# A hybrid decoder layer on one core: eight plain products in two groups of the down projection, its sums on VectorE, and the norm weight in the weight splits of the front

## The chip, the core and the metric

The kernel runs on one core of one Trainium2 chip. The metric is the device time of one launch in microseconds (us). The engines that matter are TensorE (PE in the rows; PEld are its weight loads), VectorE (DVE), ScalarE (ACT) and GpSimd (POOL). Loads and stores are DMA transfers, issued from the queue of SyncE (SP) for the most part. TensorE's clock is granted at one of two levels, 1.2 or 2.4 GHz; a stretch's granted clock is a share of full speed.

## The reference

One inference step of a decoder layer: 1024 prompt tokens and 8 sample tokens, 1024 channels, all in float32. Cut to what matters here:

```python
proj = rms_norm(h, norm_mix) @ w_in          # 1024 -> 3360; then sparse attention and gated DeltaNet
h = h + concat(o_nsa, o_gdn) @ w_out
gate, up = split(rms_norm(h, norm_ffn) @ w_gate_up)
h = h + (silu(gate) * up) @ w_down           # 2816 -> 1024, the down projection
y = rms_norm(h, norm_final)
# rms_norm(x, g) = x * rsqrt(mean(x * x) + 1e-6) * g
```

## The kernel before, in words

**Numbers.** Every operand of a large product is kept as two reduced-precision tiles, a high part (a cast on ScalarE, or a copy) and a low part (the operand less its high part). A product is then three matmuls: high by high, high by low and low by high. So each operand costs one ScalarE copy and one subtraction, and the name `split` or `parts` marks the place. `q`, `wh`/`wl`, `xh`/`xl`, `C` are such pairs.

**The front** (`in_proj`, L288 on). The 1032 tokens lie in nine tiles `x`, 128 tokens each and 8 in the last. `normalise` loads a tile, squares and sums it on ScalarE (L309), finds the root on VectorE in some eleven small instructions (`rsqrt`, L196 to L201), multiplies the tile by root and norm weight `gmix` (L319 on VectorE for the first three tiles, L316 on ScalarE and L317 on GpSimd for the others), turns it in eight TensorE transposes (L325, `S<-K,x`, `K` holding the identity) and splits the result into `xh` and `xl` (L149, L150). `natural(pw, 3)` multiplies the tiles by 352 columns of `w_in`, 24 matmuls a tile (L359), from eight weight tiles `wraw` that it loads in two pieces each and splits into `wh` and `wl`. The main program steps `normalise` and `natural` in turns. After that `conv_channels` and `channel` (L276 to L290) multiply all tokens by twelve blocks of 128 columns: one load `ch_raw` (512 KB), one copy on ScalarE (L279), one subtraction on GpSimd (L280), 72 matmuls (L285).

**The down projection** (from L2070 on). `w_down` has 22 blocks of 128 rows; blocks 1 to 20 make five groups `g` of 512 rows, and in each group four pairs `i` of two output blocks, 20 pairs `v` in all. A pair is a product of 2 by 2 blocks by 2 by 2 blocks, and it is done with seven products in place of eight (`down_pair`, `ORDER`): sums and differences of blocks are formed first, of weights in `pair_weights`, of the tokens' blocks in `group_build` (its combinations are `T1` to `T4`). Each product is 12 matmuls of 258 columns (L1874, `Z`), 84 for a pair, and after each the sum so far is added to the result `acc` (tiles `hTa`, `hTb`) on VectorE; in group 0 four of seven go to ScalarE as copies. While pair `v` runs, the weights of pair `v + 1` are split and those of `v + 2` loaded, and one step after the other of the next group's `group_build` is done: the generator `steps` hands out 14 steps in each pair.

**Who does what there.** On ScalarE the high parts. On VectorE the low parts, the adds of the results, and two of the four weight sums. On GpSimd the two other weight sums, one of seven low parts (`part(12, 6, a12, G)`), all sums of tokens' blocks (`sub(..., eng=G)`), and the residual, eight adds of 1032 columns (`res`, `RES`). `last_weights` does four low parts on GpSimd for the piece that ends the kernel, `last_down` (L1911, L1916).

**The order.** In the front a scheduler orders each engine's instructions. From the output projection on, the wrapper `InOrder` (L74) keeps those of VectorE, ScalarE and GpSimd in the order of the program, so that one that waits holds back all behind it. All three record their instructions at L74; the tiles' names tell them apart.

## Time and profile before

| | |
|---|---|
| runs of the kernel | 1840.51, 1840.69, 1845.69 us; median 1840.69 |
| profiled execution | 1840.93 us |
| its span in the trace | 1839.2 us, so 1.7 us lie outside |
| mean granted clock | 0.972 |
| busy TensorE, VectorE, ScalarE, GpSimd | 1707.1, 1129.8, 822.3, 543.1 us |

The shares are means over stages that have different limits, so the stretches are read one by one: the front up to 73 us, the conv channels up to about 240 us, and the down projection from 1543.7 to 1798.8 us. In a row, `<-` after a duration names who ended the idle time before it, `x12` counts instructions, and a form such as `128x258` is partitions by elements.

### The profile page before, as it was taken

Reading aid. Unit: us, or ns where it says so; the run is one execution under the profiler, and the core shown is the slowest. Engines: PE = TensorE matmul, PEld = TensorE weight load, DVE = VectorE, ACT = ScalarE, POOL = GpSimd, SP = SyncE. Lnnn points to the kernel's source line nnn. Section 1 sums busy time; section 2 is a strip of 40 time slices with the busy share of each in tenths; the row PEclk is TensorE's granted clock in tenths of the full one; section 3 lists DMA queues with packets and bytes.
Section 4 is the critical chain, followed back from the end, with each engine's and each line's share of the span. In section 5 each row is a group of like instructions: output and inputs, shape, how many; then the busy total and the mean of one; then the engine's idle time right before and its main releaser. Section 6 shows DMA issues by size and latency. Waiting matters only on the chain.

```text
span 1839.2 us, 32099 instructions
## 1 busy us (share of the span) xinstructions
PE 1707.1 (93%) x12066; PEld 1504.6 (82%) x12066; DVE 1129.8 (61%) x2693; ACT 822.3 (45%) x1932; POOL 543.1 (30%) x511
## 2 busy tenths in 40 slices
PE   5999999989999899999999989999999998888898
PEld 4999989989876466555486589999999998888897
DVE  6559873677467555545534268444444447899976
ACT  5357632222355665558744454433333335433322
POOL 2324330221111221110143254322333234555540
PEclk8999999999989989999999999999999999999999
DMA  7226454764422563752344342323223224332212
GB/s 212 68 92 204 163 168 123 238 207 147 107 75 61 153 201 114 191 149 87 122 139 127 85 121 78 94 88 98 86 88 104 93 82 162 104 115 81 95 55 93
DMA packets 247554, 224.02 MB, mean 122 GB/s; under 512 B 76097, under 2 KB 226113, under 8 KB 245214
## 3 DMA queue, kind: packets, MB, share of 16 engines
q1 hardware_dynamic: 232516, 189.31, 33.2%
q0 software_dynamic: 7008, 22.11, 3.7%
q10 hardware_dynamic: 7874, 10.56, 1.8%
q8 instruction: 95, 1.56, 0.4%
q14 instruction: 61, 0.50, 0.1%
HBM read 148.95 MB, written 60.40 MB: 114 GB/s over the span
## 4 chain that ended last, share of the span: by engine, by line
PE 56%; DVE 8%; DMA 5%; ACT 3%; issue 1%; POOL 1%; SPq 1%; ACTq 0%; POOLq 0%; DVEq 0%
PE X L1722 12%; PE Z L1874 7%; PE V L1722 6%; PE O L1090 4%; PE g L1495 3%; PE Y L1722 3%; DVE q L74 3%; PE mm L1420 3%; PE S L1010 2%; PE X L1097 2%; PE S L1011 2%; DMA kx<-gx 2%; PE X L1100 2%; PE X L359 1%; PE Y L1916 1%
## 5 line engine op out<-in xcount | busy, mean ns | idle before, releaser
L74 POOL TENSOR_TENSOR q<-q,q 128x258 f32<-128x258 f32 (+3 forms) x130 | 159.8, 1240 | 212.3 <-DVE q L74 184.8
L74 DVE TENSOR_TENSOR q<-q,q 128x256 fp32r<-128x256 f32 (+5 forms) x231 | 168.8, 743 | 52.3 <-ACT q L74 50.6
L74 ACT CAST q<-q 128x256 fp32r<-128x256 f32 (+2 forms) x219 | 99.3, 485 | 169.3 <-DVE q L74 158.8
L1016 ACT ACTIVATE S<-S,nb 128x512 f32<-128x512 f32 (+4 forms) x256 | 119.6, 468 | 58.7 <-DVE nb L1014 54.7
L1014 DVE TENSOR_REDUCE nb<-S 128x1 f32<-128x512 f32 (+4 forms) x154 | 95.3, 637 | 53.2 <-PE S L1013 49.1
L1102 ACT ACTIVATE PF<-X 128x512 f32<-128x512 f32 (+1 forms) x148 | 85.6, 596 | 38.9 <-PE X L1100 37.9
L359 PE MATMUL X<-wh,xl 128*128 128x320 f32 (+1 forms) x288 | 93.2, 324 | 3.3 <-DVE xl L150 3.3
L359 PE MATMUL X<-wh,xh 128*128 128x320 f32 (+1 forms) x288 | 95.4, 331 | 0.4 <-ACT xh L149 0.4
L285 PE MATMUL X<-xh,ch_h 128*128 128x344 f32 x288 | 94.7, 329 | 0.0
L359 PE MATMUL X<-wl,xh 128*128 128x320 f32 (+1 forms) x288 | 93.3, 324 | 0.3
L285 PE MATMUL X<-xh,ch_l 128*128 128x344 f32 x288 | 92.8, 322 | 0.0
L285 PE MATMUL X<-xl,ch_h 128*128 128x344 f32 x288 | 92.6, 322 | 0.0
L74 POOL TENSOR_TENSOR q<-q 128x256 f32<-128x256 f32 (+1 forms) x58 | 59.8, 1039 | 103.2 <-DVE q L74 92.6
L74 ACT COPY q<-X 128x258 f32<-128x258 f32 x80 | 30.0, 375 | 134.8 <-PE X L1722 131.2
L74 DVE TENSOR_TENSOR q<-q,Y 128x258 f32<-128x258 f32 x40 | 17.0, 424 | 118.0 <-PE Y L1722 74.4
L1462 POOL TENSOR_TENSOR wol<-woraw,woh 128x1024 fp32r<-128x1024 f32 x18 | 43.3, 2414 | 91.8 <-ACT woh L1461 91.8
L359 PEld LDWEIGHTS X<-wh,xl 128*128 128x128 f32 x288 | 55.5, 193 | 4.4 <-DVE xl L150 4.4
L359 PEld LDWEIGHTS X<-wh,xh 128*128 128x128 f32 x288 | 55.6, 193 | 1.5 <-ACT xh L149 1.1
L359 PEld LDWEIGHTS X<-wl,xh 128*128 128x128 f32 x288 | 55.6, 193 | 1.2 <-DVE wl L150 1.2
L1274 POOL DMA_INDIRECT gx<-in_cache_nsa_kv_dram,ix x32 | 30.2, 944 | 84.5 <-DMA kx<-gx 29.4
L285 PEld LDWEIGHTS X<-xh,ch_h 128*128 128x128 f32 x288 | 54.8, 190 | 0.1
L285 PEld LDWEIGHTS X<-xl,ch_h 128*128 128x128 f32 x288 | 54.7, 190 | 0.0
(766 smaller groups left out, 5623.1 us busy)
## 6 DMA issues: line engine op xcount, KB each, us to landing
q<-in_w_gate_up_dram SPq DMA_DIRECT2D x40, 512.0 KB
woraw<-in_w_out_dram SPq DMA_DIRECT2D x23, 512.0 KB
q<-g_scr SPq DMA_DIRECT2D x22, 516.0 KB
q<-in_w_down_dram SPq DMA_DIRECT2D x22, 512.0 KB
g_scr<-q SPq DMA_DIRECT2D x40, 258.0 KB
k_scr<-pack SPq DMA_DIRECT2D x8, 1280.0 KB
packr<-k_scr SPq DMA_DIRECT2D x8, 1280.0 KB
cpx<-gx SPq DMA_DIRECT2D x64, 128.0 KB
```

Of the source, the lines that this page charges most:

```text
L74: i = op(*args, **kw)
L285: mm(p[:, :CH], lhsT=a[:, k], rhs=b[:, k, CH * c:CH * c + CH], start=k == 0 and j == 0, stop=k == 7 and j == 2)
L359: mm(p[:, :ncol], lhsT=a[:, k, c0:c0 + 128], rhs=b[k][:, :ncol], start=k == 0 and j == 0, stop=k == 7 and j == 2)
L1014: V.tensor_reduce(out=nb[:, y, br, h0:h0 + per], in_=pv, op=OP.max, axis=AX.X, negate=True)
L1016: S.activation(pv[:, h], pv[:, h], AF.Exp, bias=nb[:, y, br, h0 + h:h0 + h + 1], accum_out=sm[:, y, br, h0 + h:h0 + h + 1])
L1090: x = mm(O[64 * (n % 2):64 * (n % 2) + 64], lhsT=v, rhs=pf[:w], start=n < 2, stop=n > last - 2)
L1102: S.activation(pf[:w], p[:w], AF.Exp)
L1420: mm(p, lhsT=a(k), rhs=b(k), start=k == 0 and j == 0, stop=k == n - 1 and j == 2)
L1462: (eng or G).tensor_tensor(wl, raw, wh.bitcast(F32), op=OP.subtract)
L1495: mm(p[:, :n], lhsT=x[:, k], rhs=y[:, :n], start=i == 0 and j == 0, stop=i == 7 and j == 2)
L1722: mm(p, lhsT=w[n][:, x, c], rhs=y[:, k, 258 * q:258 * q + 258], start=new and k == 0 and j == 0, stop=k == nk - 1 and j == 2, skip_group_c ...
L1874: mm(p[:, q], lhsT=w[n][:, x, c], rhs=y[:, k, 258 * q:258 * q + 258], start=new and k == 0 and j == 0, stop=k == 1 and j == 2, skip_group_ ...
```

## The change

In the front the norm weight no longer goes onto the tokens. It is loaded as eight rows, turned once on TensorE and kept as a column per block (`gain`); the weight splits multiply by it (ScalarE with a scale, VectorE in one instruction with two operations), and `channel` multiplies `ch_raw` by it in eight ScalarE instructions. The root goes into the turning of the tiles: in place of a transpose against the identity it is a float32 matmul against `dg`, the identity times the root. All loads of this part are issued in a new order, written out by hand.

In the down projection groups 1 and 3 (`straight`) take eight plain products in a pair: 96 matmuls, four adds of results, no sums of blocks, four low parts of weights. What GpSimd did there goes to VectorE. The residual comes in two loads at the starts of groups 0 and 2 and is added in groups 1 and 3.

```diff
     K = con.tile([128, MD], F32, name="K")
-    ld(K[:, :128], A['c_f32'][:, :128])
-    ld(K[:, 128:], A['c_f32'][:, 128:MD])
     ident, ones, uinc = K[:, ID:ID + 128], K[:, ONE:ONE + 128], K[:, UIN:UIN + 128]
     identr = con.tile([128, 128], F32R, name="identr")
-    V.tensor_copy(identr, ident)
     identb = con.tile([128, 128], BF, name="identb")
-    V.tensor_copy(identb, ident)
+    gain = con.tile([128, 8], F32, name="gain")
...
         ld(raw, w_in[:, col:col + 128].rearrange("(k p) c -> p k c", p=128))
+        for k in range(8):
+            S.mul(raw[:, k], raw[:, k], gain[:, k:k + 1])
         S.copy(wh, raw)
...
+        def normalise(px, xt):
+            v = px.tile([128, 3], F32, name="v")
+            V.memset(v, 1.0)
+            for i, (n, c0, x) in enumerate(xt):
+                sq = px.tile([128, D], F32, name="xsq", bufs=1)
+                S.activation(sq[:n], x[:n], AF.Square, accum_out=v[:n, i:i + 1])
+            m = len(xt)
+            V.tensor_scalar(v[:, :m], v[:, :m], 1.0 / D, EPS, op0=OP.mult, op1=OP.add)
+            y = rsqrt(px, v[:, :m], [128, m], f"x{m}")
+            for i, (n, c0, x) in enumerate(xt):
+                dg = px.tile([128, 128], F32, name="dg", bufs=3)
+                V.tensor_scalar(dg, ident, y[:, i:i + 1], None, op0=OP.mult)
+                for k4 in range(2):
+                    p = bank("tp")
+                    pv = p.rearrange("p (k t) -> p k t", k=4)
+                    for k in range(4):
+                        kk = 4 * k4 + k
+                        mm(pv[:, k, :n], lhsT=x[:n, 128 * kk:128 * kk + 128], rhs=dg[:n, :n], start=True, stop=True)
+                    split(xh[:, 4 * k4:4 * k4 + 4, c0:c0 + n], xl[:, 4 * k4:4 * k4 + 4, c0:c0 + n], pv[:, :, :n])
...
-                split(h[:, :ncol], l[:, :ncol], raw[:, :ncol])
+                S.activation(h[:, :ncol], raw[:, :ncol], AF.Copy, scale=gain[:, k:k + 1])
+                V.scalar_tensor_tensor(l[:, :ncol], raw[:, :ncol], gain[:, k:k + 1], h[:, :ncol].bitcast(F32),
+                                       op0=OP.mult, op1=OP.subtract)
...
+            c_rope = A['c_rope'][:T].rearrange("(t p) c -> p t c", p=128)
+            xt = load(px, (0,))
+            ld(K[:, :128], A['c_f32'][:, :128])
+            g8 = px.tile([8, 128], F32, name="g8", bufs=1)
+            ld(g8, A['norm_mix'].rearrange("l (k p) -> (l k) p", p=128))
+            V.tensor_copy(identr, ident)
+            V.tensor_copy(identb, ident)
+            p = bank("tp")
+            tr(p[:, :8], g8, ident[:8, :8])
+            V.tensor_copy(gain, p[:, :8])
+            loaded = raw_weights(natural_columns(3), range(4))
+            xt += load(px, (1,))
+            loaded += raw_weights(natural_columns(3), range(4, 8))
+            ld(rope[:, :2], c_rope[:, :2])
+            xt += load(px, (2, 3))
+            ld(K[:, 128:], A['c_f32'][:, 128:MD])
+            xt += load(px, (4, 5))
+            ld(rope[:, 2:8], c_rope[:, 2:8])
             ld(rope[:NB, 8], A['c_rope'][T:])
-            for _ in range(4):
-                next(gates)
-            for n in norm:
-                if not sv:
-                    sv.update(m=1)
-                    tmp = px.tile([128, 768], F32, name="masktmp", bufs=1)
-                    ld(tmp, A['c_f32'][:, MD:])
+            xt += load(px, (6, 7, 8))
+            tmp = px.tile([128, 768], F32, name="masktmp", bufs=1)
+            ld(tmp, A['c_f32'][:, MD:])
+            normalise(px, xt[:1])
+            gates = natural(pw, 3, loaded)
+            for a, b in ((1, 2), (2, 3), (3, 4), (4, 6), (6, 9)):
+                if a == 4:
                     G.tensor_copy(maskb, tmp)
-                for _ in range(4 * n):
+                normalise(px, xt[a:b])
...
+    def plain_parts(w, *blocks):
+        plan = {}
+        for n, a in enumerate(blocks):
+            parts(plan, 3 * n, lambda n=n: [w[n][:, x].rearrange("p (k c) -> p k c", c=128) for x in range(2)], a, V)
+        return run(plan, 12)
...
+        if straight(g):
+            for n, (b, src) in enumerate((((0, 0), b11), ((1, 0), b21), ((0, 1), b12), ((1, 1), b22))):
+                part(8 * n, b, src)
+            return run(plan, 28)
...
-        def sub(step, o, a, b, eng=G):
+        def sub(step, o, a, b, eng=G if spare is not None else V):
...
+    def straight_pair(C, w, acc, m, prep):
+        for x in range(2):
+            for h in range(2):
+                p = ps_now[0].tile([128, 2, 512], F32, name="Z", bufs=4)[:, :, :258]
+                for q in range(2):
+                    for k2 in range(2):
+                        bh, bl = C[k2, h]
+                        for k in range(2):
+                            c = slice(128 * k, 128 * k + 128)
+                            for j, (y, b) in enumerate(((0, bh), (0, bl), (1, bh))):
+                                mm(p[:, q], lhsT=w[2 * x + k2][:, y, c], rhs=b[:, k, 258 * q:258 * q + 258],
+                                   start=k2 == 0 and k == 0 and j == 0, stop=k2 == 1 and k == 1 and j == 2)
+                        next(prep, None)
+                a = acc(m + x, slice(HN * h, HN * h + HN)).rearrange("p (q n) -> p q n", q=2)
+                V.tensor_tensor(a, a, p, op=OP.add)
...
-                    wp = pair_weights(w_next, *a)
+                    wp = plain_parts(w_next, *a) if straight((v + 1) // 4) else pair_weights(w_next, *a, G=V)
...
+                    if g in (0, 2):
+                        res = [combo(pools, b, 1, [128, 2, NT], F32) for b in ("T4", "T1")]
+                        for x in range(2):
+                            o = 2 * g + 2 * x
+                            ld(res[x], h_scr[o:o + 2].rearrange("m p n -> p m n"))
                     if g < 4:
-                        res = combo(pools, "T4", (g + 1) % 2, [128, 2, NT], F32)
-                        ld(res, h_scr[2 * RES_OF[g]:2 * RES_OF[g] + 2].rearrange("m p n -> p m n"))
...
-                down_pair(C[g], w, acc, 2 * i, steps(), g == 0)
+                if straight(g):
+                    straight_pair(C[g], w, acc, 2 * i, steps())
+                else:
+                    down_pair(C[g], w, acc, 2 * i, steps(), g == 0)
                 for _ in wp:
                     pass
                 if i == 3:
                     last += list(build)
-                if (g, i) in RES:
-                    for m in range(2):
-                        a_, r_ = acc(2 * RES[g, i] + m, slice(0, NT)), res[:, m]
-                        G.tensor_tensor(a_, a_, r_, op=OP.add)
+                if straight(g):
+                    a_ = acc(2 * g - 2 + i, slice(0, NT))
+                    V.tensor_tensor(a_, a_, res[i // 2][:, i % 2], op=OP.add)
```

**SP's queue at the start.** Before, the constants `K`, the first token tile, the norm weight on all partitions (`gmix`) and the rotary table lie ahead of the weights `wraw`:

```order
L167 DMA K<-in_c_f_dram 128x128
L168 DMA K<-in_c_f_dram 128x440
L305 DMA x<-in_x_prompt_dram 128x1024
L307 DMA gmix<-in_norm_mix_dram 128x1024
L438 DMA rope<-in_c_rope_dram 128x8x128
L439 DMA rope<-in_c_rope_dram 8x128
L337 DMA wraw<-in_w_in_dram 128x344
```

and now:

```order
L303 DMA x<-in_x_prompt_dram 128x1024
L446 DMA K<-in_c_f_dram 128x128
L448 DMA g_126<-in_norm_mix_dram 8x128
L335 DMA wraw<-in_w_in_dram 128x344
L335 DMA wraw<-in_w_in_dram 128x8
L335 DMA wraw<-in_w_in_dram 128x344
L335 DMA wraw<-in_w_in_dram 128x8
L335 DMA wraw<-in_w_in_dram 128x344
L335 DMA wraw<-in_w_in_dram 128x8
L335 DMA wraw<-in_w_in_dram 128x344
L335 DMA wraw<-in_w_in_dram 128x8
L303 DMA x<-in_x_prompt_dram 128x1024
```

The first tile moved from third to first, the second tile from behind all eight weights to behind four of them, and the tables behind the weights.

**VectorE in group 1.** The first pair of the group, while blocks for group 2 are built (`b00h`, `b10h`, `b11h`; `hTa<-hTa,Z` adds a result, `q<-q` are weights or loaded blocks). Before:

```order
L74 TENSOR_TENSOR b00h<-q_17388,b00h 128x516
L74 TENSOR_TENSOR q_17513<-q_17383,q_17513 128x256
L74 TENSOR_TENSOR b10h<-q_17389,b10h 128x516
L74 TENSOR_TENSOR b10h<-q_17390,b10h 128x516
L74 TENSOR_TENSOR hTa<-hTa,Z 128x516
L74 TENSOR_TENSOR q_17383<-q_17383 128x2x128
L74 TENSOR_TENSOR b11h<-q_17389,b11h 128x516
L74 TENSOR_TENSOR b11h<-q_17390,b11h 128x516
L74 TENSOR_TENSOR hTa<-hTa,Z 128x516
```

and now:

```order
L74 TENSOR_TENSOR hTa<-hTa,b01l 128x1032
L74 TENSOR_TENSOR b00h<-q_17452,b00h 128x516
L74 TENSOR_TENSOR b00h<-q_17453,b00h 128x516
L74 TENSOR_TENSOR q_17579<-q_17450,q_17579 128x256
L74 TENSOR_TENSOR b10h<-q_17454,b10h 128x516
L74 TENSOR_TENSOR b10h<-q_17455,b10h 128x516
L74 TENSOR_TENSOR q_17452<-q_17452 128x516
L74 TENSOR_TENSOR q_17453<-q_17453 128x516
L74 TENSOR_TENSOR b11h<-q_17454,b11h 128x516
L74 TENSOR_TENSOR b11h<-q_17455,b11h 128x516
L74 TENSOR_TENSOR hTa<-hTa,Z 128x516
```

The sums of blocks (`q_17452<-q_17452 128x516`) and the residual (`hTa<-hTa,b01l 128x1032`) came from GpSimd, and fewer adds of results stand between. GpSimd has no instruction left from the second pair's weights on.

**SP's queue where the down projection begins.** `g_scr` holds the tokens' blocks, `h_scr` the residual. Before:

```order
L2095 DMA b01l<-h_scr 128x2x1032
L158 DMA g_scr<-q_16473 256x1x258 x2
L1854 DMA q_16856<-in_w_down_dram 128x4x256
L1788 DMA q_16860<-g_scr 128x1032
L1788 DMA q_16861<-g_scr 128x1032
```

and now:

```order
L2147 DMA T1l<-h_scr 128x2x1032
L1890 DMA q_16960<-in_w_down_dram 128x4x256
L158 DMA g_scr<-q_16577 256x1x258 x2
L2147 DMA b01l<-h_scr 128x2x1032
L1820 DMA q_16966<-g_scr 128x1032
L1820 DMA q_16967<-g_scr 128x1032
```

One of two loads of the residual now stands right ahead of the loads of group 1's blocks, and the load of weights is ahead of the stores.

## Rows read from the trace of the kernel before

**Rows 1.** Busy time by stretch of the down projection: the stretch in us, its length, then busy us (and instructions) of PE, PEld, DVE, ACT and POOL, the granted clock, the DMA share and GB/s.

```profile
1543.72:1798.80 255.08, 218.35 (x1684) 213.22 (x1683) 227.42 (x341) 90.79 (x213) 132.85 (x104) 0.95 0.29 100
...
1600.00:1640.00 40.00, 32.25 (x248) 31.18 (x247) 36.87 (x51) 12.95 (x32) 24.14 (x18) 0.96 0.22 73
1680.00:1720.00 40.00, 32.94 (x257) 32.24 (x256) 38.50 (x57) 12.59 (x31) 22.77 (x17) 0.96 0.38 131
```

**Rows 2.** Who TensorE waited for from 1543 to 1800 us: total us, times, longest.

```profile
PE Z L1874 <- DVE hTa L74: 15.4, 13, 3.3
PE Z L1874 <- DVE hTb L74: 13.5, 4, 4.4
PE Z L1874 <- ACT hTa L74: 4.6, 3, 2.7
PE Z L1874 <- ACT hTb L74: 3.2, 1, 3.2
```

**Rows 3.** From the chain of waits (start us, us, what): a piece of group 1 in which group 2's blocks are built, and the end of the down projection.

```profile
1626.85 3.92 DVE T1h L74 x2
...
1774.39 24.41 PE Z L1874 x180
1798.80 0.44 PE Y L1911 x4
```

**Rows 4.** VectorE's instructions by line and form from 1535 to 1800 us: busy us, mean ns | idle before. Then VectorE in time while GpSimd has nothing to do.

```profile
L74 DVE TENSOR_TENSOR q<-q,q 128x256 fp32r<-128x256 f32 x117 | 80.9, 701 | 3.3 <-ACT q L74 3.2
L74 DVE TENSOR_TENSOR hTa<-hTa,Z 128x516 f32<-128x516 f32 x62 | 42.3, 685 | 11.0 <-PE Z L1874 10.5
L74 DVE TENSOR_TENSOR T1h<-q,T1h 128x516 fp32r<-128x516 f32 x6 | 9.8, 1677 | 0.0
...
1784.44 0.69 DVE L74 TENSOR_TENSOR hTb<-hTb,Z 128x516 f32<-128x516 f32 x1
1785.05 0.42 DVE L74 TENSOR_TENSOR q<-q 128x256 f32<-128x256 f32 x1
1785.39 0.42 DVE L74 TENSOR_TENSOR q<-q,q 128x256 fp32r<-128x256 f32 x1
```

**Rows 5.** TensorE in time: the first and the last of 34 matmuls of 258 columns in the gate and up projection, and the first products of the down projection and three of its waits.

```profile
1499.81 0.29 PE L1722 MATMUL X<-T1l,hTb 128*128 128x258 f32 x1
...
1503.90 0.40 PE L1722 MATMUL X<-b00h,q 128*128 128x258 f32 x2
...
1543.72 1.62 PE L1874 MATMUL Z<-b00h,q 128*128 128x258 f32 x12
...
1549.46 1.70 PE L1874 MATMUL Z<-T2h,q 128*128 128x258 f32 x12 [2.70 <-ACT hTa L74]
...
1562.65 1.71 PE L1874 MATMUL Z<-T2h,q 128*128 128x258 f32 x12 [1.34 <-ACT hTa L74]
```

**Rows 6.** ScalarE in the same place.

```profile
1545.51 0.62 ACT L74 CAST b01h<-q 128x516 fp32r<-128x516 f32 x1 [3.47 <-POOL q L74]
...
1557.55 0.62 ACT L74 CAST b00l<-q 128x516 fp32r<-128x516 f32 x1 [0.63 <-DMA q<-g_scr]
```

**Rows 7.** The front in time: an SP issue, ScalarE's first square, the root's first and last instruction, the first transposes and products, the last weights, the second tile.

```profile
7.24 1.06 ACT L309 ACTIVATE xsq<-x 128x1024 f32<-128x1024 f32 x1 [1.04 <-DMA x<-in_x_prompt_dram]
...
8.42 0.15 DVE L312 TENSOR_SCALAR v<-v 128x1 f32<-128x1 f32 x1 [5.38 <-ACT xsq L309]
...
10.54 1.28 DVE L319 SCALAR_TENSOR_TENSOR x<-x,rs_yx,gmix 128x1024 f32<-128x1024 f32 x1
...
11.88 1.97 PE L325 MATMUL S<-K,x 128*128 128x128 f32 x8 [11.88 <-DMA wraw<-in_w_in_dram]
...
13.67 0.66 PE L359 MATMUL X<-wh,xh 128*128 128x352 f32 x1
...
16.32 0.43 SPq L305 DMA_DIRECT2D x<-in_x_prompt_dram  x1
...
18.88 0.53 DVE L150 TENSOR_TENSOR wl<-wraw,wh 128x352 fp32r<-128x352 f32 x1 [0.35 <-ACT wh L149]
...
20.72 1.06 ACT L309 ACTIVATE xsq<-x 128x1024 f32<-128x1024 f32 x1 [1.88 <-DMA x<-in_x_prompt_dram]
...
25.67 1.97 PE L325 MATMUL S<-K,x 128*128 128x128 f32 x8 [5.63 <-DVE v L312]
...
57.97 1.47 PE L325 MATMUL S<-K,x 128*128 128x128 f32 x12
...
72.77 3.63 PE L767 MATMUL g<-cmp_pet,cmp_w 128*128 128x2 f32 x32
```

**Rows 8.** Float32 matmuls that are no transposes: in time, eight and what follows them, and all of their line (in the program 32 calls, four heads in eight chunks).

```profile
128.53 1.14 PE L537 MATMUL S<-K,ga 128*128 128x128 f32 x8
129.43 0.40 PE L285 MATMUL X<-xh,ch_h 128*128 128x344 f32 x1
...
L537 PE MATMUL S<-K,ga 128*128 128x128 f32 x64 | 8.9, 282 | 0.0
```

**Rows 9.** ScalarE in the conv channels: a copy of 128 columns in the front (busy us, mean ns), and busy time of all engines by stretch, columns as in rows 1.

```profile
L389 ACT COPY nat<-X 128x128 f32<-128x128 f32 x8 | 2.2, 273 | 0.0
...
73.00:115.00 42.00, 42.00 (x272) 41.70 (x272) 24.63 (x66) 15.43 (x29) 6.75 (x5) 0.96 0.21 67
...
125.00:150.00 25.00, 23.76 (x165) 23.44 (x164) 18.02 (x51) 18.53 (x28) 5.80 (x4) 1.00 0.41 127
150.00:175.00 25.00, 25.00 (x177) 24.95 (x176) 22.55 (x63) 19.39 (x27) 13.88 (x11) 1.00 0.67 242
```

More of the change, by code (lines that the diff above doesn't have):

```diff
@@ new lines, in tokens, with load @@
+        def tokens(t):
+            return (xp[128 * t:128 * t + 128], 128, 128 * t) if t < 8 else (xs, NB, T)
+        def load(px, ts):
+            out = []
+            for t in ts:
+                src, n, c0 = tokens(t)
+                x = px.tile([128, D], F32, name="x", bufs=9)
+                ld(x[:n], src)
+                out.append((n, c0, x))
+            return out
+        def normalise(px, xt):
[17 more added lines that the diff above has]
+                    split(xh[:, 4 * k4:4 * k4 + 4, c0:c0 + n], xl[:, 4 * k4:4 * k4 + 4, c0:c0 + n], pv[:, :, :n])
@@ L329, in in_proj, with raw_weights @@
         anchor, raws = [None], []
-        def weights(pw, cols, ncol):
-            wh, wl = [], []
-            for k in range(8):
+        def raw_weights(cols, ks):
+            out = []
+            for k in ks:
                 raw = raws[-1].tile([128, 352], F32, name="wraw", bufs=8 if len(raws) == 1 else 5)
@@ L1789, in group_raw, with straight @@
         return r
-    POOLED = ()
+    def straight(g):
+        return g % 2 == 1
     def group_build(pools, r, g, C, spare=None):
@@ L1810, in lo @@
                 for k in range(2):
[L1811 to L1812 removed]
+                    V.tensor_tensor(C[b][1][:, k], src[k], C[b][0][:, k].bitcast(F32), op=OP.subtract)
             plan.setdefault(step, []).append(hi)
             plan.setdefault(step + (1 if spare is not None else 3), []).append(lo)
[L1817 removed]
+        def sub(step, o, a, b, eng=G if spare is not None else V):
             def f():
@@ L1858, in down_tiles @@
         t = [(tw if x == 13 else gw).tile([128, 2, 2, 256], F32R, name=f"q{x}")
-             for x in ((13, 11, 12, 10) if v % 2 else (4, 5, 6, 7))]
-        return [t[n // 2][:, n % 2] for n in range(7)]
+             for x in ((13, 11, 12, 10) if v % 2 else (4, 5, 6, 7))[:2 if straight(v // 4) else 4]]
+        return [t[n // 2][:, n % 2] for n in range(4 if straight(v // 4) else 7)]
+    def straight_pair(C, w, acc, m, prep):
[13 more added lines that the diff above has]
+                V.tensor_tensor(a, a, p, op=OP.add)
     def down_pair(C, w, acc, m, prep, first):
```

59 lines of the change are left out of this document (14 added, 45 removed).

## The prediction, written before the changed kernel ran

> **What bounds the kernel now.** I read the busy time by stretch first, then who TensorE waited for in the stretches where it is not full, then the duration of single forms, the chain of waits and the order in time. The change touches two stages.
>
> In the down projection TensorE is busy for 218 of 255.1 us, with VectorE at 227 of 255 and at 36.87 and 38.50 of 40 in the middle [rows 1]. TensorE's waits sum to 36.7 us (15.4 + 13.5 + 4.6 + 3.2), 28.9 of them for VectorE's adds of results [rows 2]. The reader is to see that VectorE is full there because its instructions are long, not because they are many. A low part of 256 columns takes 0.34 us from start to start, an add of 516 columns 0.61, where GpSimd is idle beside them (1784.44 to 1785.39); the means over the stage are 0.70 for the first and 1.68 for `T1h` of 516 columns [rows 4]. Adds that read a result take 0.685 on average, as they do undisturbed: only those with both operands in SBUF stretch. In group 1 two `T1h` fill 3.92 us of the chain [rows 3], while GpSimd is at work for 132.85 us of the stage [rows 1].
>
> The stage's floor: 34 matmuls of 258 columns went by in 4.09 us (1499.81 to 1503.90), 0.1203 each [rows 5]. 20 pairs of 84 are 1680, 202.1 us. Lost are 53.0: 36.7 of waits, about 12.8 by the granted clock (0.95 instead of 1 over 255 us [rows 1]), 3.5 the rest.
>
> In the front the first turning starts at 11.88 and its tile is done near 20; then TensorE waits 5.63 us until 25.67, because the second tile landed at 20.72. SyncE issued its load at 16.32 only, behind sixteen pieces of weights [rows 7]. Later (from 73 us) TensorE is full, 42.00 of 42 us [rows 9], so what the front gains goes straight to the end.
>
> **The down projection.** Added: groups 1 and 3 have 8 pairs of 96 instead of 84 matmuls: 96 x 0.1203 = 11.5 us, floor 213.6. Removed: three of seven result adds a pair, the weight sums there and all of GpSimd's work beside VectorE. What VectorE must do afterwards, at the undisturbed pace of rows 4: in an odd group 16 result adds x 0.61, 23 weight instructions x 0.34 (three pairs of 4, one of 11), 22 block sums and low parts x 0.61 for the next group, 4 residual adds of 1032 columns at an estimated 1.15 (the slope from 256 to 516 columns continued): 9.8 + 7.8 + 13.4 + 4.6 = 35.6 us, beside 4 x 96 x 0.1203 = 46.2 of TensorE. In an even group 28 x 0.61 + 37 x 0.34 + 8 x 0.61 = 34.5 beside 40.4. So TensorE becomes the bound in every group, with a slack of six to ten us for what arrives late. Waits for VectorE's adds should nearly vanish. If the pace were that of the means in rows 4, the same counts would make about 74 and 58 us, and VectorE would bind: that is the other end, and a rival below.
>
> Kept: the wait of 2.70 us at 1549.46, since ScalarE's cast behind it waited 3.47 for a sum of GpSimd that the change leaves there [rows 5, 6]. The wait of 1.34 at 1562.65 hangs on a cast that waits for `g_scr`, 0.63 [rows 6]; ahead of that load now stands 1.05 MB of residual, so I take 4 in place of 1.34 (1.3 if other queues carry it, 6.5 if it all stands ahead at some 200 GB/s). With half a us for odd ones, waits of 7; a clock of 0.99, 2.5; the rest as before, 3.5. Stage: 213.6 + 13.0 = 226.6, that is 28.5 less than 255.1. Bounds: 217 if no wait is left, 240 if half of the waits and clock loss stay.
>
> **The front.** Removed: the multiplication of each tile (1.28 us on VectorE at 10.54 for the first) and the wait for the second tile. Added: `dg`, 0.2 to 0.4 us a tile, and float32 matmuls in place of transposes. The row of such matmuls has 64 records for 32 calls, eight records in 0.90 us (128.53 to 129.43), so 0.225 for one; twelve transposes took 1.47, 0.122 each [rows 7, 8]. 72 of them: 72 x 0.103 = 7.4 us more. At the low clock the first eight need some 3.6 to 3.9 us instead of the 1.8 from 11.88 to 13.67.
>
> The Trainium skill, "TensorE: Matmul & The Clock Gate", section "Terms", says that the transpose mode is four times faster for float32. This case's trace shows 1.85 times, 0.225 against 0.122, for matmuls of the same size. By the page the turnings would cost 72 x 3 x 0.122 = 26 us more; I use the row, and keep the page's case as a rival.
>
> Now the start. Before, the first square could run at 7.24, with 0.8 MB landed and the load issued third [rows 7]. The tile is first now: 0.9 us earlier by the issue, up to 1.4 more by 0.28 MB less at 200 GB/s, so 5.0 to 6.3, taken as 5.5. Square 1.06, root 2.1 (8.42 to 10.54), two weight low parts of 352 columns on VectorE between them, about 0.44 each (the slope of rows 4), and `dg` 0.25: turning can start at about 10.2, and the first product at 14.1, against 13.67. No gain there. The other weights lie ahead of the tables now, and the second tile behind four weights instead of behind eight, which puts it at about 11 instead of 20.7. So tile 0 ends at about 17 (20 before) and the second turning follows without the 5.63. From there: seven tiles of 24 x 0.16 + 8 x 0.225 = 5.64 us and a small one of 4.7, 44.2, plus 5.2 us of waits for low parts and low clock that I leave in: 66.4 in place of 72.77. Gain 6.4. Bounds: 13 gained, if clock and waits go as well; 6 lost, if the weights stay where they were and the turnings run at the low clock.
>
> **The conv channels.** Twelve blocks with eight ScalarE multiplications of 128x128: 96, with the nearest row at 273 ns for a copy of that form [rows 9], 26 us. ScalarE is at 18.53 and 19.39 of 25 us where the blocks come [rows 9]; the 26 us spread over the 165 from 73 us to 240 make some 8 more in those 50, which fit, and the splits run ahead of their use by several us. Cover gone, TensorE would wait for the last part of some blocks: 0 to 8, taken as 2. The weight splits with a factor keep their count and form: nothing, hidden beside 42.00 of 42 us of TensorE.
>
> **Sum**, against the profiled execution of 1840.93 (span 1839.2 and 1.7 around it), which is 0.24 above the median of the runs: -28.5 - 6.4 + 2 = -32.9, so **1808 us**.
>
> **Rivals.**
> 1. *The down projection gains half.* VectorE keeps program order; an add of 1032 columns or two block sums ahead of a result add hold its bank, and with four banks `Z` TensorE stops. For it: VectorE waits for nothing at 36.87 of 40 us [rows 1]; against it: ten us of slack in an odd group. Stage 240, total 1821.
> 2. *The front gives nothing*: VectorE's weight parts ahead of `dg` delay the root, or the second tile still lands late. Total 1808 + 6.4 = 1814; with the lower bound, 1820.
> 3. *The turnings cost the fourfold.* The row at 0.225 speaks against it. 26 - 7.4 = 19 more: 1827. The page named above is the one that says so.
> 4. *Slower.* The length of VectorE's instructions is its own (operands, not GpSimd beside it). Then the moved sums and 22 block instructions take the mean of 1.68 and 0.70, and VectorE's load over five groups is 2 x 74 + 3 x 58 = 322 instead of 2 x 35.6 + 3 x 34.5 = 175. It decides from about half-way between (248 plus waits of 7 is the 255 of before); at six tenths it makes 263 + 7, some 15 over, less the front's 4: 1852. Against it: the pair 0.34 and 0.70 of one form in rows 4, and that adds from PSUM do not stretch.
>
> **Chances.** Forecast 0.62, its own range 1797 to 1818; rival 1 0.15; rival 2 0.13; rival 3 0.03; rival 4 0.04; better than the forecast's range 0.03. The range for 8 in 10, from the bounds of stage and front, is 1793 to 1823. A measurement here tells a difference of 0.3%, 5.5 us, from none. All cases but rival 4 and the worst of 1 lie below 1835: faster 0.94, same 0.02, slower 0.04.
>
> **What would show it.** Right: GpSimd idle from the first pairs on; VectorE's low parts near 0.34 and `T1h` near 0.61; 1776 matmuls `Z`; the stage 220 to 233 us long with under 12 us of waits; the second turning at 17 to 18; the first gate products at about 66 in place of 72.77; two records and 0.225 us for a float32 turning; conv multiplications near 0.27 with TensorE full beside them. Wrong: low parts still at 0.7 with GpSimd idle; waits on `hTa` and `hTb` still above 18 us; a second turning after 22; turnings of 0.49 each.

## The result: 1794.9 us, and the profile after

The changed kernel took 1794.9 us (median of four runs, 1792.78 to 1799.33) against 1841.8 (four runs, 1840.51 to 1845.69): a ratio of 0.9745, 95% interval 0.9721 to 0.9769. The forecast was 1808, range 1793 to 1823; the measurement lies in that range, but below the 1797 to 1818 that the prediction gave as the forecast's own. The profiled execution took 1795.02 us, its span 1793.3, so 45.9 us less span than before.

First the down projection. Busy time by stretch (length, then busy us of PE, PEld, DVE, ACT, POOL, granted clock, DMA share, GB/s), the stage as a whole; it answers to [rows 1]:

```profile
1533.20:1752.30 219.10, 215.77 (x1779) 214.86 (x1778) 173.33 (x334) 76.93 (x177) 3.53 (x3) 0.99 0.33 113
```

The stage is 35.9 us shorter (255.0 to 219.1). TensorE is busy for nearly all of it, VectorE for 79% in place of 89%, GpSimd not at all after its last 3.5 us. Who TensorE waited for there, the answer to [rows 2]:

```profile
PE Z L1926 <- ACT hTa L74: 3.0, 1, 3.0
PE Z L1926 <- DVE hTa L74: 0.3, 1, 0.3
```

36.7 us of waits became 3.3. VectorE's instructions by form (busy us, mean ns, idle before), to be held against [rows 4]:

```profile
L74 DVE TENSOR_TENSOR q<-q,q 128x256 fp32r<-128x256 f32 x109 | 44.8, 417 | 6.3 <-ACT q L74 6.3
L74 DVE TENSOR_TENSOR hTa<-hTa,Z 128x516 f32<-128x516 f32 x50 | 34.1, 686 | 19.5 <-PE Z L1908 14.4 <-PE Z L1926 4.9
L74 DVE TENSOR_TENSOR hTb<-hTb,Z 128x516 f32<-128x516 f32 x49 | 33.6, 686 | 19.0 <-PE Z L1926 10.8 <-PE Z L1908 8.0
...
L74 DVE TENSOR_TENSOR T1h<-q,T1h 128x516 fp32r<-128x516 f32 x6 | 5.0, 866 | 0.0
```

A low part of 256 columns takes 417 ns where it took 701, `T1h` 866 where it took 1677, and the adds that read a result 686, as before (685). And the idle time stands on the other side now: VectorE's adds are idle before them for 38.5 us over the two tiles, nearly all of it waiting for TensorE (23.2 before), where TensorE waited for them.

Then the front. TensorE in time: the turnings of the first four tiles, the first product and the last product of the front; it answers to [rows 7]:

```profile
9.90 3.79 PE L324 MATMUL S<-dg,x 128*128 128x128 f32 x16 [5.26 <-DVE dg L318]
13.34 0.64 PE L368 MATMUL X<-wh,xh 128*128 128x352 f32 x1
...
18.39 2.05 PE L324 MATMUL S<-dg,x 128*128 128x128 f32 x16 [0.17 <-DVE dg L318]
...
23.51 2.02 PE L324 MATMUL S<-dg,x 128*128 128x128 f32 x16
...
26.66 1.95 PE L324 MATMUL S<-dg,x 128*128 128x128 f32 x16
...
65.02 0.32 PE L368 MATMUL X<-wh,xl 128*128 128x352 f32 x1
```

The wait of 5.63 us for the second tile is gone: 0.17 is left, and no other wait follows up to 65 us. The product that was the last of the front at 72.61 before starts at 65.02.

Where the 45.9 us lie, by landmarks that both kernels have (the front's last product, the first turning of the conv state, and the first and the last `Z`):

| | before | after | gain in the stretch |
|---|---|---|---|
| last product of the front | 72.61 | 65.02 | 7.6 |
| turning of the conv state | 241.57 | 236.39 | -2.4 |
| first product of the down projection | 1543.7 | 1533.2 | 5.3 |
| its end (first turning of the last piece) | 1798.6 | 1752.3 | 35.9 |
| span | 1839.2 | 1793.3 | -0.4 |

### The profile page after: what moved, and what is told of

Read it like the earlier page. It is cut to its first block, busy times and chain, and to the rows that moved or that the text cites. A ratio compares the mean times of both kernels' runs of the same rounds, so it can differ in the third digit from the quotient of the medians.

```text
span 1793.3 us, 32292 instructions
## 1 busy us (share of the span) xinstructions
PE 1706.5 (95%) x12235; PEld 1511.2 (84%) x12235; DVE 1070.3 (60%) x2693; ACT 833.3 (46%) x1986; POOL 399.2 (22%) x404
## 4 chain that ended last, share of the span: by engine, by line
PE 59%; DMA 6%; DVE 3%; ACT 3%; issue 2%; POOL 1%; SPq 1%; POOLq 0%; ACTq 0%; DVEq 0%
PE X L1752 13%; PE Z L1926 6%; PE V L1752 6%; PE Z L1908 5%; PE O L1114 4%; PE g L1519 4%; PE Y L1752 3%; PE mm L1444 2%; PE S L1034 2%; DMA kx<-gx 2%; DMA gx<-in_cache_nsa_kv_dram,ix 2%; PE X L1121 2%; PE X L368 2%; PE S L1035 2%; PE g L809 2%
## 5 line engine op out<-in xcount | busy, mean ns | idle before, releaser
L74 DVE TENSOR_TENSOR q<-q,q 128x256 fp32r<-128x256 f32 (+5 forms) x234 | 138.4, 606 | 51.9 <-ACT q L74 50.4
L74 ACT CAST q<-q 128x256 fp32r<-128x256 f32 (+2 forms) x195 | 90.3, 495 | 129.8 <-DVE q L74 78.9
L1711 POOL TENSOR_TENSOR q<-q,q 128x512 f32<-128x512 f32 x40 | 58.9, 1473 | 133.7 <-DVE q L74 106.0
L74 POOL TENSOR_TENSOR q<-q,q 128x258 f32<-128x258 f32 (+1 forms) x44 | 45.2, 1038 | 50.4 <-DVE q L74 50.4
L284 PEld LDWEIGHTS X<-xh,ch_l 128*128 128x128 f32 x288 | 55.1, 191 | 0.0
```

The lines of the kernel that those rows point to most:

```text
L74: i = op(*args, **kw)
L284: mm(p[:, :CH], lhsT=a[:, k], rhs=b[:, k, CH * c:CH * c + CH], start=k == 0 and j == 0, stop=k == 7 and j == 2)
L1711: plan.setdefault(step, []).append(lambda: eng.tensor_tensor(out, x, y, op=op))
```

## The experiments

The theory of the prediction had two halves: GpSimd at work beside VectorE stretches VectorE's instructions, and the down projection waits for VectorE; and the second tile's late load held the front. The first four runs take the change apart: front or down projection alone, and within the down projection plain products without the move of the sums, and the move without the plain products.

**The down projection alone** (against the changed kernel; the whole front and the conv channels as before):

```diff
-                dg = px.tile([128, 128], F32, name="dg", bufs=3)
-                V.tensor_scalar(dg, ident, y[:, i:i + 1], None, op0=OP.mult)
+                        V.scalar_tensor_tensor(x, x, y[:, i:i + 1], gmix, op0=OP.mult, op1=OP.mult)
...
-                S.activation(h[:, :ncol], raw[:, :ncol], AF.Copy, scale=gain[:, k:k + 1])
+                split(h[:, :ncol], l[:, :ncol], raw[:, :ncol])
```

> The change of the down projection alone; front and conv channels as before. Of the 46.9 us that the whole change gave, the traces put 36.0 on the down projection (255.1 to 219.1 us), 5.2 on all up to 240 us, and some 5 on the stretch between, which the change does not touch. Theory: the parts add up and the stretch between varies from run to run: 1802 to 1806. Rival: what is gained in the stretch between comes with the front (later loads fall otherwise): then 1805 to 1808 here and 1831 in the run of the front alone. Rival two: part of the front's gain is needed for the gain of the down projection or the other way round: above 1808.

1801.7 us, ratio 0.9806 (0.9782 to 0.9831), 0.3 us below the theory's 1802 to 1806. Its stage is 218.1 us long (219.1 in the changed kernel), and TensorE's waits there are the same two (3.0 and 0.3).

**The front alone** (against the changed kernel; the whole down projection as before):

```diff
-                    wp = plain_parts(w_next, *a) if straight((v + 1) // 4) else pair_weights(w_next, *a, G=V)
+                    wp = pair_weights(w_next, *a)
...
-                if straight(g):
-                    straight_pair(C[g], w, acc, 2 * i, steps())
-                else:
-                    down_pair(C[g], w, acc, 2 * i, steps(), g == 0)
+                down_pair(C[g], w, acc, 2 * i, steps(), g == 0)
```

> The change of the front and the conv channels alone; the down projection as before. Theory (parts add up): 5 us less than before, 1835 to 1838, with the second turning at 18.4 and the last product of the front at about 65 us. Rival: the front carries the gain between as well: 1830 to 1832.

1833.9 us, ratio 0.9976 (0.9964 to 0.9989), that is 4.4 us less by the ratio and 5.4 by the medians; the time lies between the theory's 1835 to 1838 and the rival's 1830 to 1832, and settles neither. The last product of its front starts at 66.57, its down projection is 252.7 us long with the waits of before. The two ratios multiply to 0.978, against 0.9745 (0.9721 to 0.9769) and, in a second measurement below, 0.9766 (0.9745 to 0.9787): the parts add up within what these runs tell, and neither needs the other.

**Plain products, and GpSimd keeps its share** (the four last low parts too):

```diff
-                    wp = plain_parts(w_next, *a) if straight((v + 1) // 4) else pair_weights(w_next, *a, G=V)
+                    wp = plain_parts(w_next, *a) if straight((v + 1) // 4) else pair_weights(w_next, *a)
-        def sub(step, o, a, b, eng=G if spare is not None else V):
+        def sub(step, o, a, b, eng=G):
-                    V.tensor_tensor(a_, a_, res[i // 2][:, i % 2], op=OP.add)
+                    G.tensor_tensor(a_, a_, res[i // 2][:, i % 2], op=OP.add)
```

> The changed kernel, groups 1 and 3 as plain products, but GpSimd keeps what it had: the block sums, two weight sums and a low part of each seven-product pair, the residual, the four last low parts. If GpSimd's work beside VectorE is what stretched its instructions: low parts of 256 columns at 0.55 to 0.7 again on average, waits for VectorE's adds back in part, stage 232 to 248 us in place of 219, total 1808 to 1824. Rival (fewer adds and no sums for two groups are what gave the time, whoever does the rest): within 4 us of the changed kernel, 1791 to 1799.

1801.3 us, ratio 0.9797 (0.9775 to 0.9819); stage 223.3 us. The theory's price was too high: it named 232 to 248 for the stage and 1808 to 1824 in all; the rival's 1791 to 1799 was missed by 2.3 us (in a second measurement below the changed kernel itself takes 1798.1). Its first sign came true all the same. VectorE by form, the stage as a whole, and who TensorE waited for:

```profile
L74 DVE TENSOR_TENSOR q<-q,q 128x256 fp32r<-128x256 f32 x98 | 63.3, 661 | 6.3 <-ACT q L74 5.9
...
L74 DVE TENSOR_TENSOR T1h<-q,T1h 128x516 fp32r<-128x516 f32 x6 | 9.4, 1611 | 0.0
```

```profile
1536.00:1759.30 223.30, 216.25 (x1778) 214.96 (x1778) 178.99 (x274) 77.59 (x177) 86.92 (x64) 0.99 0.33 112
```

```profile
PE Z L1926 <- ACT hTa L74: 3.0, 1, 3.0
PE Z L1926 <- DVE hTa L74: 1.9, 2, 1.6
PE Z L1926 <- ACT q L74: 1.4, 1, 1.4
PE Z L1926 <- DVE hTb L74: 0.7, 2, 0.4
```

The instructions are as long as before (661 for 701, 1611 for 1677), with GpSimd busy for 86.92 us. So who works beside VectorE does set its pace. But TensorE's waits are 7.0 us in all, not 36.7: VectorE is busy for 179 of 223 us, and an engine with a fifth of its time free can be slow in single instructions and still be in time.

**Seven products everywhere, all on VectorE** (against the kernel with the front alone changed; the residual's loads as before):

```diff
-                    wp = pair_weights(w_next, *a)
+                    wp = pair_weights(w_next, *a, G=V)
-        def sub(step, o, a, b, eng=G):
+        def sub(step, o, a, b, eng=G if spare is not None else V):
-                        G.tensor_tensor(a_, a_, r_, op=OP.add)
+                        V.tensor_tensor(a_, a_, r_, op=OP.add)
-                G.tensor_tensor(t[:, 1], raw, t[:, 0].bitcast(F32), op=OP.subtract)
+                V.tensor_tensor(t[:, 1], raw, t[:, 0].bitcast(F32), op=OP.subtract)
```

> The changed front, and in the down projection seven products in all groups, with all sums and low parts on VectorE. VectorE's work by group at its undisturbed paces: group 0 about 38, groups 1 to 3 some 17.1 + 15.0 + 13.4 + 2.5 = 48, group 4 about 31, against 40.4 for TensorE. Theory: VectorE binds in three groups, 40.4 + 3 x 48 + 40.4 + 4 = 229 us, total 1803 to 1808; GpSimd's absence gives three quarters of the stage's gain, the plain products the rest. Rival: plain products are needed for nearly all of it, since results that come late stop TensorE: stage 240 or more, total over 1816. Other rival: they give nothing (VectorE keeps up): 1783 to 1792, since 11.5 us of matmuls are saved.

1818.0 us, ratio 0.9897 (0.9871 to 0.9924); stage 238.6, in a profiled execution of 1811.2 us. TensorE's waits of over a us, VectorE by form, and the stage:

```profile
PE Z L1898 <- DVE hTa L74: 9.3, 11, 1.6
PE Z L1898 <- DVE hTb L74: 8.7, 6, 3.4
PE Z L1898 <- ACT hTa L74: 4.3, 2, 3.0
```

```profile
L74 DVE TENSOR_TENSOR q<-q,q 128x256 fp32r<-128x256 f32 x133 | 54.9, 415 | 2.1 <-ACT q L74 2.1
```

```profile
1530.10:1768.70 238.60, 214.66 (x1682) 208.16 (x1681) 221.69 (x442) 90.23 (x213) 3.70 (x3) 0.98 0.31 107
```

VectorE has its full pace (415 ns), and is full all the same: 221.69 of 238.6 us, with 23.8 us of waits left in all. It is the reverse of the run before: fast instructions, but too many. Between theory (229) and first rival (240 or more) the stage lies nearer to the rival, and the total is the rival's (over 1816). With the front's stage of 252.7 us as the start, moving the sums alone gives 14.1, the plain products alone 29.4, both together 33.6; the theory had given the move three quarters of the gain. The two overlap, since both take from VectorE's load (226.4 us before, 221.7 with the move, 179.0 with the plain products): behind the plain products the move has 4.2 us left to give, behind the move the plain products 19.5.

**Plain products in group 3 alone:**

```diff
     def straight(g):
-        return g % 2 == 1
+        return g == 3
```

(the residual comes in three loads at the start of group 2 and one in group 3, and is added in groups 3 and 4.)

> The changed kernel with plain products in group 3 alone; group 1 by seven products, all on VectorE; the residual in groups 3 and 4. 48 matmuls fewer, 5.8 us. VectorE's work at the undisturbed paces: group 1 some 45.5 us beside 40.4 of TensorE, the other groups 31 to 38. Theory: one group in which VectorE binds costs about what the matmuls give (in the run with three such groups TensorE waited some 24 us, 8 for each, less the 3 at the start): stage 217 to 222 us, total 1791 to 1798, within 4 of the changed kernel. Rival: the neighbours' slack absorbs it: stage 214 to 216, total 1788 to 1791. Rival two: late adds pile up: over 1800.

1803.6 us, ratio 0.9799 (0.9764 to 0.9835); its stage is 223.9 us, where 217 to 222 was expected and the changed kernel has 219.1. TensorE's waits there:

```profile
PE Z L1926 <- DVE hTa L74: 4.6, 4, 2.5
PE Z L1926 <- ACT hTa L74: 3.0, 1, 3.0
PE Z L1926 <- DVE hTb L74: 1.7, 2, 1.1
```

5.8 us of matmuls were saved, and there are 6.0 us more of waits for VectorE (6.3 for 0.3) and a mean clock of 0.98 for 0.99; these make 221.5, and 2.4 us of the stage are left without a name. VectorE is busy for 197.6 of 223.9 us. Where the waits lie: 3.7 us in group 1, as the theory says, where VectorE is busy for 43.59 of 46.11 us (1589.56 to 1635.67); but the longest wait lies in group 4, behind two residual adds that this edit had moved there:

```profile
1735.51 2.37 DVE L74 TENSOR_TENSOR hTb<-hTb,b01l 128x1032 f32<-128x1032 f32 x2
...
1739.68 2.03 PE L1926 MATMUL Z<-T2h,q 128*128 128x258 f32 x12 [2.48 <-DVE hTa L74]
```

The granted clock is 0.79 from 1738 to 1746, which loses another 1.7 us. Without this wait and this loss the stage would be some 219.7 us, much like the changed kernel's 219.1, so the second plain group by itself is not shown to pay. The total lies above both the theory's 1791 to 1798 and what the stage explains; the rest stands in the untouched stretch, of which more below.

**The load order of the front:**

```diff
-            loaded = raw_weights(natural_columns(3), range(4))
+            loaded = raw_weights(natural_columns(3), range(8))
             xt += load(px, (1,))
-            loaded += raw_weights(natural_columns(3), range(4, 8))
```

> The changed kernel with one load moved: the second token tile behind all eight weights of the front, not behind four. In the changed kernel it is issued at 6.68, its square starts at 12.49 and its turning at 18.39. Theory: it lands at 15 to 16, the square ends near 17, the root takes 2.1 to 4.4 us behind the weights' low parts: second turning at 20 to 22, 2 to 4 us more in all, 1796 to 1799. Rival: the root was held up by the low parts anyway, and the later tile is not late: second turning before 19.5, no difference. Rival two: the wait costs the granted clock too, as in the kernel before (0.74 from 20 to 40 us): 5 us or more.

1803.7 us, ratio 0.9803 (0.9772 to 0.9833). The scatter below forbids to read a few us from the total; the trace of the front can be read. The first two turnings:

```profile
9.95 3.79 PE L324 MATMUL S<-dg,x 128*128 128x128 f32 x16 [5.10 <-DVE dg L318]
...
20.37 3.67 PE L324 MATMUL S<-dg,x 128*128 128x128 f32 x16 [2.73 <-DVE v L314]
```

The second turning comes 2.0 us later, after 2.73 of idle time, and then takes 3.67 us for the same sixteen records that took 2.05: TensorE's clock had fallen, and from 20 to 30 us it was granted 0.83 where the changed kernel has 1.00. The front's last product starts at 68.33, 3.3 us later. That is the theory, with a part of the second rival: here the late tile cost its wait, and 1.6 us more in a turning at half rate.

**Transposes in the front, the root on ScalarE:**

```diff
-                dg = px.tile([128, 128], F32, name="dg", bufs=3)
-                V.tensor_scalar(dg, ident, y[:, i:i + 1], None, op0=OP.mult)
+                S.mul(x[:n], x[:n], y[:n, i:i + 1])
...
-                        mm(pv[:, k, :n], lhsT=x[:n, 128 * kk:128 * kk + 128], rhs=dg[:n, :n], start=True, stop=True)
+                        tr(pv[:, k, :n], x[:n, 128 * kk:128 * kk + 128], ident[:n, :n])
```

> The changed kernel, but the tiles are multiplied by the root on ScalarE (1024 columns, some 1.05 us each) and turned by transposes, not by float32 matmuls against the identity times the root. Theory: TensorE has no waits from 18 to 66 us in the changed kernel, so 72 turnings that are 0.10 us cheaper give 72 x 0.10 = 7 us, less one for the later first turning: 1787 to 1790. Rival: the multiplication lies in the chain from the tile's landing to its turning, and waits for it take the place of the longer turning: 1793 to 1797. Rival two: TensorE's clock is granted worse after transposes: granted clock under 0.9 between 20 and 40 us, as in the kernel before, and over 1797.

1798.4 us, ratio 0.9781 (0.9754 to 0.9808): not told apart from the changed kernel. In the trace the front's last product starts at 60.71, 4.3 us earlier and not 7; the first turning waits longer and new waits appear for ScalarE:

```profile
10.65 1.97 PE L323 MATMUL S<-K,x 128*128 128x128 f32 x8 [6.07 <-ACT x L317]
...
18.18 1.09 PE L323 MATMUL S<-K,x 128*128 128x128 f32 x8 [0.57 <-ACT x L317]
20.27 0.43 PE L367 MATMUL X<-wh,xh 128*128 128x352 f32 x1 [0.99 <-ACT xh L149]
```

The granted clock fell too, to 0.83 from 20 to 30 us and 0.91 from 20 to 40, where the second rival named under 0.9. At the conv state's turning 0.9 us is left of the 4.3 (235.46 for 236.39).

**No norm weight in the conv channels:**

```diff
-        for k in range(8):
-            S.mul(raw[:, k], raw[:, k], gain[:, k:k + 1])
```

> The changed kernel without the eight multiplications by the norm weight in each of the twelve blocks of the conv channels (that part of the norm weight is left out of the computation). Theory: the front's gain shrank from 7.4 us at 75 us to 5.2 at 240, so the 96 multiplications cost about 2: 1791 to 1794. Rival: they are hidden, and the shrinking comes from elsewhere: no difference. Rival two: their 31.6 us on ScalarE cost more than the predicted 2, up to 8: below 1790.

1794.9 us, ratio 0.9755 (0.9724 to 0.9785): not told apart by its time. Its conv state is turned at 235.55 after a front that ends at 64.87. Five kernels with the unaltered front and conv channels of the changed one reach that point at 236.3 to 239.5 with fronts that end between 64.79 and 65.07 (66.57 and 239.30 in the sixth). Between these two points the mean granted clock is 0.98 in those at 236 and in the kernel without the multiplications, and 0.97 in those at 239. So the 96 multiplications cost TensorE 0.8 to 0.9 us by kernels of like clock, and 3.6 to 4.0 by the others. Even without them the stretch takes 170.7 us, 1.7 more than before (169.0), where the clock was 0.99. They are 395 ns each, not 273:

```profile
L277 ACT ACTIVATE ch_raw<-ch_raw,gain 128x128 f32<-128x128 f32 x96 | 31.6, 395 | 10.7 <-DMA ch_raw<-in_w_in_dram 10.7
```

(the changed kernel, ScalarE by form from 20 to 240 us.)

**The changed kernel again, and two tries to better it.** The three ran beside each other. The second puts the multiplication of the conv weights on GpSimd, the third takes the transposes as well:

```diff
-        for k in range(8):
-            S.mul(raw[:, k], raw[:, k], gain[:, k:k + 1])
+        G.tensor_tensor(raw, raw, gain[:, :, None].to_broadcast([128, 8, 128]), op=OP.mult)
```

> The changed kernel once more, unaltered, beside the next two on the same chip. Theory: the stretch from 240 us to the down projection, which no edit touches, scatters by some us from run to run and from chip to chip (it began the down projection at 1533.2 in the changed kernel and at 1539.0 in the run without the conv multiplications, with fronts that ended together): 1793 to 1801, a down projection of 219 us, a front that ends near 65. Rival: the 1794.9 of the first measurement hangs on that chip's luck alone: 1800 or more, all of it between 240 us and the down projection.

> The changed kernel, but the norm weight goes onto the conv channels' weights in one GpSimd multiplication of 1024 columns a block, not in eight on ScalarE. Theory: the eight multiplications (31.6 us in all, 395 ns each) delay the casts of the decay and key stage that TensorE waits for; with them off ScalarE 2 to 4 us less than the unaltered kernel beside it. Rival: twelve instructions of some 2.5 us that read two operands stretch VectorE, which is at 22.55 of 25 us there, and cost as much: no difference, or up to 5 more.

> The run before it, and the front's tiles multiplied by the root on ScalarE and turned by transposes. In the trace of that front alone the last product of the front ended 4.3 us earlier than in the changed kernel (60.71 for 65.02), while its time was 1798.4 in another call. Theory: 3 to 5 us less than the run before it, 5 to 8 less than the unaltered kernel. Rival: what the front gains is lost by 240 us to ScalarE and to the granted clock: within 2 us of the run before it.

Unaltered: 1798.1 us, ratio 0.9766 (0.9745 to 0.9787), with a down projection of 219.4 us and a last product of the front at 65.07, as its theory says. With the multiplication on GpSimd: 1803.3, 0.9805 (0.9779 to 0.9831). With the transposes too: 1802.1, 0.9791 (0.9769 to 0.9813). Neither beats the changed kernel. Busy time of the kernel with the GpSimd multiplication where the conv channels run (columns as above):

```profile
125.00:150.00 25.00, 22.06 (x144) 21.74 (x143) 18.11 (x50) 14.78 (x20) 11.98 (x9) 0.93 0.44 152
150.00:175.00 25.00, 25.00 (x176) 24.93 (x176) 24.38 (x61) 18.46 (x26) 14.60 (x9) 1.00 0.56 197
```

ScalarE is relieved, but TensorE's waits for it (`pack`) stay at 3.5 us. VectorE goes to 24.38 of 25 us, and to 144.2 us from the front's end to the conv state's turning, for 125.0 in the unaltered kernel; TensorE waits 2.9 us for a VectorE instruction (`kn`) that cost it 1.3 in the changed kernel. The conv state is turned at 240.05 in place of 236.47. That is the rival of this run for the greater part: 0.6 of these 3.6 us stood at the front's end (65.67 for 65.07), and the clock from there on is 0.97 for 0.98. With the transposes the conv state is turned at 233.97, 2.5 us ahead of the unaltered kernel, so what the front gained is not lost by 240 us, as the rival of that run has it, but behind.

The repeated kernel also tells what a difference of a few us is worth. From the conv state's turning to the first `Z`, a stretch that no edit touches, these kernels needed:

| kernel | us |
|---|---|
| before | 1302.1 |
| changed, first and second profile | 1296.8, 1300.9 |
| front alone, GpSimd keeps its share, all on VectorE, one plain group (same front) | 1299.0, 1296.5, 1293.8, 1304.2 |
| down projection alone (front of before) | 1298.8 |
| other load order, no conv multiplication, transposes | 1300.1, 1303.5, 1307.0 |
| GpSimd multiplication, and with transposes | 1304.1, 1307.0 |

Among six with the same front it spans 10.5 us. Most of the scatter goes with TensorE's granted clock. The nine executions of the changed kernel show it: those with a mean clock of 0.979 to 0.981 took 1798.1 to 1799.3 us, those with 0.982 to 0.986 took 1792.0 to 1795.0. In the stretch itself TensorE's busy time, for the same matmuls, goes from 1232.9 us (all on VectorE) to 1243.8 (GpSimd multiplication), while its idle time is 60.8 and 60.4. Both with transposes stand at 1307, with the most idle time of all (64 and 66); whether these edits cost something there stays open, since each has one profile.

## Why the prediction held, point by point

**Floor of the down projection**: held. 1776 matmuls at 0.1203 are 213.6; with 3.3 of waits and 0.01 of the clock, 2.2, that makes 219.1, what the stage measured. The 3.5 us that the prediction kept as a rest are not there. By the prediction's own sum the 35.9 us gained are, to 0.1, 33.4 of waits, 10.6 of the clock (12.8 lost before at 0.95, 2.2 now) and the 3.5, less 11.5 of added matmuls: with the waits most of the clock's loss went too.

**Waits for VectorE**: they vanished as said, and VectorE's load was near what was worked out: 173 us of busy time for 175. The undisturbed pace came back (417 ns as a duration; the 0.34 us of the prediction are from start to start). The Trainium skill says in "GPSIMD Engine Reference", section "Specifications", that GpSimd's SBUF interfaces are shared with VectorE, with contention for VectorE instructions with two SBUF inputs. The traces agree: 661 and 701 ns with GpSimd at work, 415 and 417 without, and 685 against 686 for adds that take one operand from PSUM.

**The reason given for it** was only half of it. The prediction let the gain hang on the pace ("because its instructions are long, not because they are many"). The run with GpSimd's share kept has the slow pace and 4.2 us more of stage; the run with the full pace and seven products keeps 23.8 us of waits. By these kernels what decides is VectorE's load against the stage: at 227 of 255 and 222 of 239 TensorE waits for it (28.9 and 18.9 us), at 198 of 224 for 6.3, at 179 of 223 and 173 of 219 for 2.6 and 0.3. The move to VectorE is worth 14 us by itself and 4 behind the plain products.

**The wait of 4 us behind the residual's load**: this is the term that failed most plainly, as "I take 4 in place of 1.34". There is no such wait. ScalarE in the changed kernel at that place:

```profile
1546.77 0.62 ACT L74 CAST b00l<-q 128x516 fp32r<-128x516 f32 x1
1547.85 0.63 ACT L74 CAST b00l<-q 128x516 fp32r<-128x516 f32 x1 [0.46 <-DMA q<-g_scr]
1548.38 0.58 ACT L74 COPY hTa<-Z 128x516 f32<-128x516 f32 x1
...
1549.71 0.59 ACT L74 COPY hTa<-Z 128x516 f32<-128x516 f32 x1 [0.44 <-PE Z L1926]
1551.14 0.59 ACT L74 COPY hTa<-Z 128x516 f32<-128x516 f32 x1 [0.84 <-PE Z L1926]
```

One cast still waits 0.46 for `g_scr`. But the next block's casts no longer stand behind it: in a plain group the parts of `group_build` are spread eight steps apart, at 0, 8, 16 and 24, in place of 0, 1 and 2, so ScalarE's copies of results follow at once, and they wait for TensorE. The spacing stood in the diff and was not read. The kernel with the down projection alone changed bears this out. Its two casts wait for `g_scr` as they did before (0.62 and 0.63 there), with the residual's load ahead:

```profile
1553.14 0.62 ACT L74 CAST b00l<-q 128x516 fp32r<-128x516 f32 x1 [0.62 <-DMA q<-g_scr]
1554.43 0.63 ACT L74 CAST b00l<-q 128x516 fp32r<-128x516 f32 x1 [0.67 <-DMA q<-g_scr]
```

TensorE has no wait there. So the residual made no load later, and as far as these kernels tell the spacing took the wait away. In the kernel with one plain group the parts of group 1 stand at 0, 1 and 2 again, but no cast waits for `g_scr`, and TensorE does not wait either: so the wait seems to take both, late loads and casts close together.

**The wait at the start** (2.70 kept): 3.02, held.

**The front**: first square at 5.25 for 5.5, first product at 13.34 for 14.1, second turning at 18.39 for 17 to 18, the end 7.6 us earlier for 6.4 (the gate products, by which the prediction set its 66.4, start at 66.37, but three other pieces stand ahead of them now). The place of the second tile's load alone is worth 3.3 of that by the run that moved it. The float32 turning cost what its row said: sixteen records from 18.39 to 20.22, 1.83 us for eight, 0.229 each for 0.225. The Trainium skill's factor of four ("TensorE: Matmul & The Clock Gate", section "Terms") does not show: 0.229 against 0.122 is 1.9. Undoing the float32 turning gave 4.3 of 7.4 us: ScalarE's multiplication came into the chain, and the clock fell to 0.83 from 20 to 30 us.

**The conv channels**: 2 forecast, 2.4 between the landmarks. That this agrees is in part luck: by the run without the multiplications they cost 0.8 to 0.9 us at a like clock, and the other 1.7 are there without them. They took 395 ns and not the 273 of the nearest row, which read PSUM and was a plain copy, and was a poor neighbour.

**What was not in the sum**: 5.3 us between 240 us and the down projection. By the table above this is within what that stretch scatters, for the most part with the granted clock; the second profile of the same kernel has 1.2 of it.

So 13 us separate the forecast from the first measurement: 7.4 in the down projection (waits and rest kept too high), 5.3 of scatter, 0.8 in front and conv channels together. By the second measurement (1798.1) 10 are left.

**The rivals**: "the down projection gains half" describes the run with all sums on VectorE, not the changed kernel. "The front gives nothing" fell by the trace, "the fourfold" by the row of the turnings, and the slower one by the pace in the changed kernel: VectorE's length was not its own.

## What to carry to other kernels

Before moving work between two engines that disturb each other, add up each engine's work against the time of the one that should bind: here lowering the count (plain products, fewer adds and sums) brought 29.4 us, ending the disturbance by moving the work 14.1, and once the lower count had made slack, the move was worth 4.2. A little more work on the binding engine can pay when it takes far more off the one that it waits for: 11.5 us more of matmuls, with the move of the sums, took away 33.4 us of waits, and 10.6 of what the clock had lost. Where edits meant to save a few us change an order early in a long program, read the stage that they touch in the trace, since the total scatters by more.

## What the runs showed of the hardware that was not expected

TensorE's clock: an idle time of 2.73 us in the front was followed by a turning at half rate (3.67 us for 2.05) and a granted clock of 0.83 from 20 to 30 us; in the kernel before, the 5.63 us of idle time lie in a stretch, 20 to 40 us, that was granted 0.74. With 0.17 us of idle time it stayed at 1.00. So the waits of 2.73 and 5.63 us cost more than their length.

A ScalarE multiplication of 128 columns by a column of factors took 395 ns, a copy of the same form from PSUM 272. And an add of 1032 columns took 1.23 us on VectorE and 2.6 to 2.8 on GpSimd.
